# Moving some stores of a two-layer encoder kernel to ScalarE's queue, with three small re-stagings of its side work

## The chip, the cores and the metric

One core of one Trainium2 chip. The metric is the device time of one execution in microseconds (us), as the median of the runs shown.

## The reference

Two residual layers and a final RMSNorm over 1024 tokens of 1024 channels, all in fp32. Cut to what matters:

```python
for l in range(DEPTH):                       # 2
    h = rms_norm(x, norm_g[l])
    proj = h @ w_in[l]                       # 1024 x 6912
    qA, kA, vA, zA, uB, vB, zB, qM, zM, g_logits = split(proj)
    yA = gqa_axial_attention(qA, kA, vA, ...) * silu(zA)      # 8 query heads, 2 key heads, rotary
    yB = chunked_spatial_gating(uB, vB, ...) * silu(zB)       # layer norm, 128 x 128 mixing
    mem_n = rms_norm(mem, mem_norm_g[l])                      # 256 memory rows
    yM = memory_cross_attention(qM, mem_n, w_mem_kv[l]) * silu(zM)
    up = einsum('bsnw,nwd->bsnd', stack([yA, yB, yM]), w_br[l])
    x = x + sum(sigmoid(g_logits) * up, axis=2) @ w_out[l]
return rms_norm(x, final_g)
```

## The kernel before

Every large product is made of three fp32r matmuls (`mm3`, lines 122 to 124): each operand is split by ScalarE (a cast, the high part) and by VectorE or GpSimd (a subtraction, the low part). `split_w` (lines 164, 165) does this for weights, `split` (132, 133) for activations, `turn` (127) is a transpose on TensorE.

**Opening.** For each layer, `memory` norms 256 memory rows (L150, L152), turns them in four groups of four (two for each half of the rows), splits the results into `mTh` and `mTl`, multiplies by the key and value weights and stores the result in DRAM. Each group of turns takes a PSUM bank from `psT`, a pool of two; `psM` and `psA` are one bank each and are not used at this point. The token rows are normed and turned in between.

**Input projection** (`in_proj`). 27 column blocks of 256, each as seven products of 12 matmuls (a Winograd form of Strassen's scheme), 189 products in a written order. The weight operands are made seven products ahead (`AHEAD`); a block's weights are one load of 1 MB (`get_raw`). A block's results go through `use`, which is of a kind for each block: the last 12 blocks are gate logits (`logit`: a tanh on ScalarE, L405, and a store to `g_d`, 256 KB, four for each block); queries of the memory branch (`parts`) are stored in two parts to `qm_d`.

**Side work.** Between the products, `in_proj` resumes generators at given product numbers: `side` is a list of (start, generator), and a `yield n` means "go on n products later"; at most two generators are resumed behind one product. `qkv(L, tt)`, one for each of eight blocks of 128 rows, starts at 27 + 9 tt: it loads queries and keys from `proj_d`, turns them 4 products later (copies L560, L565), applies norm and rotary positions, splits (casts L586, L589 on ScalarE, subtractions L592, L594 on VectorE), turns the keys (copy L601, two stores of 128 KB to `k_d`), and one product later turns both groups of queries (copy L610 and a store of 256 KB to `qs_d` for each). The two groups and the keys share the two `psT` banks. `spatial(L, tt)` starts at 103 + 9 tt: it loads `vt` and `uz`, and 4 products later turns `vt` and goes through layer norm (copy L656), mixing and gating.

**After the projection.** Eight products before its end `cross` begins to load for the memory attention: keys and values (`kv_d`) and the queries of the first unit (`qm_d`); then come the loads of `yb_d` (4 MB), the keys and values of the other heads and the queries of the second unit. Its score matmuls are L766, L767 and L769. Then follow attention, the three branches (L723 multiplies by a gate that is loaded from `g_d`) and the output projection.

**What sets the order.** TensorE's order is the program's. The other engines' queues are ordered by a scheduler at build time, by readiness and priority (`tc.high_priority` raises it); buffers come from pools, of which `b2` has 18 and is used by nearly all side work and stores. Every DMA, load or store, is issued by `dma` on SyncE's queue (L106), in order: one that waits holds those behind it.

Of the kernel before, what the change touches and what calls it, by code (L numbers as in the profile page):

```python
# [28 lines left out]
NT = T // P  # L29
# [21 lines left out]
def trunk(ctx, tc, x_in, mem, norm_g, w_in, q_norm_g, k_norm_g, sg_ln_g, sg_ln_b, w_s, b_s,  # L51
          mem_norm_g, w_mem_kv, w_br, w_out, final_g, rope_t, out):
    nc = tc.nc
# [51 lines left out]
    def dma(out, in_):  # L105
        nc.sync.dma_start(out=out, in_=in_)  # L106

    eye = b2()[:, :P]
    make_identity(nc, eye)
    identr = const.tile([P, P], F32R, name="identr")  # L110
# [69 lines left out]
    def memory(l):  # L180

        gb = wt((P, D), F32)
        rows = slab((P, 2, D), F32)
        dma(rows[:, 0], mem[0, :P])
        dma(gb, mem_norm_g[l].partition_broadcast(P))
        dma(rows[:, 1], mem[0, P:2 * P])
        yield
        for mt in range(2):
            rms_rows(rows[:, mt], gb)
        mTh, mTl = slab((P, KT, MEM)), slab((P, KT, MEM))  # L190
        for mt in range(2):
            for i in range(2):
                pt = psT()
                for j in range(4):
                    turn(pt[:, j * P:(j + 1) * P], rows[:, mt, (4 * i + j) * P:(4 * i + j + 1) * P])
                m = slice(mt * P, (mt + 1) * P)
                k = slice(4 * i, 4 * i + 4)
                split(mTh[:, k, m], mTl[:, k, m], pt.rearrange("p (k t) -> p k t", k=4))
        yield
        for n in range(4):  # L200
            raw = raw_kv.pop(0)
            get_kv()
            W = [split_w(raw[:, i:i + 2], nc.vector if i % 4 else nc.gpsimd) for i in range(0, KT, 2)]
            for j in range(2):
                ps = psB()[:, :256]
                c = slice(j * P, (j + 1) * P)
                for kt in range(KT):
                    wh, wl = W[kt // 2]
                    if n < 2:
                        mm3(ps, wh[:, kt % 2, c], wl[:, kt % 2, c], mTh[:, kt], mTl[:, kt], kt == 0, kt == KT - 1)  # L210
                    else:
                        mm3(ps, mTh[:, kt, c], mTl[:, kt, c], wh[:, kt % 2], wl[:, kt % 2], kt == 0, kt == KT - 1)
                s = b2(F32R, (P, 2, 256))
                split(s[:, 0], s[:, 1], ps)
                if n < 2:
                    dma(kv_d[l][2 * n + j, :, :2].rearrange("p a m -> p a m"), f32(s))
                else:
                    for h in range(2):
                        dma(kv_d[l][2 * (n - 2) + h, :, 2:, c], f32(s[:, :, h * P:(h + 1) * P]))
            yield  # L220
# [139 lines left out]
    def blocks(L):  # L360

        def silu2(z):
            t = b2()
            nc.scalar.activation(t, z, AF.Tanh, scale=0.5)
            nc.vector.scalar_tensor_tensor(out=t, in0=t, scalar=1.0, in1=z, op0=ALU.add, op1=ALU.mult)
            return t

        def keep(dst):
            def use(j, th, z, bank):
                if bank:  # L370
                    t = b2()
                    nc.scalar.copy(t, z)
                    z = t
                dma(dst[j][:, half(th)], z)
            return use

        def gate(dst):
            def use(j, th, z, bank):
                dma(dst[j][:, half(th)], silu2(z))
            return use  # L380

        def both(dst):
            got = {}

            def use(j, th, z, bank):
                got[j, th] = z
                if (0, th) in got and (1, th) in got:
                    a = silu2(got[1, th])
                    u = got[0, th]
                    (nc.gpsimd if th else nc.vector).tensor_tensor(out=a, in0=a, in1=u, op=ALU.mult)  # L390
                    dma(dst[:, half(th)], a)
            return use

        def parts(dst):
            def use(j, th, z, bank):
                h, lo = b2(F32R), b2(F32R)
                split(h, lo, z, lo=nc.vector if bank else nc.gpsimd)
                dma(dst[j][:, 0, half(th)], f32(h))
                dma(dst[j][:, 1, half(th)], f32(lo))
            return use  # L400

        def logit(dst):
            def use(j, th, z, bank):
                t = b2() if bank else z
                nc.scalar.activation(t, z, AF.Tanh, scale=0.5)  # L405
                dma(dst[j][:, half(th)], t)
            return use

        out = [(K0, V0, keep(L.proj[4:6]))]
        out += [(Q0 + i * 256, Q0 + i * 256 + P, keep(L.proj[2 * i:2 * i + 2])) for i in range(2)]  # L410
        out += [(UB0 + f * P, ZB0 + f * P, both(L.uz[f])) for f in range(4)]
        out += [(VB0 + i * 256, VB0 + i * 256 + P, keep(L.proj[6 + 2 * i:8 + 2 * i])) for i in range(2)]
        out += [(ZA0 + i * 256, ZA0 + i * 256 + P, gate(L.za[2 * i:2 * i + 2])) for i in range(2)]
        out += [(QM0 + i * 256, QM0 + i * 256 + P, parts(L.qm[2 * i:2 * i + 2])) for i in range(2)]
        out += [(ZM0 + i * 256, ZM0 + i * 256 + P, gate(L.zm[2 * i:2 * i + 2])) for i in range(2)]
        out += [(G0 + i * 256, G0 + i * 256 + P, logit(L.g[2 * i:2 * i + 2])) for i in range(12)]
        return out
# [131 lines left out]
    def qkv(L, tt):  # L549

        t = slice(tt * P, (tt + 1) * P)
        qt, kt = b2(F32, (P, 4, P)), b2(F32, (P, 2, P))
        dma(qt, L.proj[0:4, :, t].rearrange("f p t -> p f t"))
        dma(kt, L.proj[4:6, :, t].rearrange("f p t -> p f t"))
        yield 4
        pt = psT()
        for f in range(2):
            turn(pt[:, f * P:(f + 1) * P], kt[:, f])
        kr = b2()
        nc.scalar.copy(kr[:, :256], pt[:, :256])  # L560
        pt = psT()
        for f in range(4):
            turn(pt[:, f * P:(f + 1) * P], qt[:, f])
        qr = b2()
        nc.scalar.copy(qr, pt)  # L565
        yield 1
        v = kr[:, P:2 * P].rearrange("p (g d) -> p g d", g=2)
        vs = b2(F32R, (P, 2, 2, 64))
        nc.scalar.copy(vs[:, :, 0], v)
        tabk, tabq = tabs[0]  # L570
        tmp = b2()
        k = Rope(kr[:, :P], tabk, 2, tt, tmp[:, :P], tmp[:, P:2 * P])
        q = Rope(qr, tabq, 8, tt, b2(), b2())
        k.begin()
        q.begin()
        yield 1
        nc.vector.tensor_tensor(out=vs[:, :, 1], in0=v, in1=f32(vs[:, :, 0]), op=ALU.subtract)
        dma(L.v[:, :, tt], f32(vs).rearrange("p g s d -> p g (s d)"))
        q.turn()
        k.turn()  # L580
        yield 1
        q, k = q.end(), k.end()
        yield 1
        ks = b2(F32R, (P, 2, 2, 2, 64))
        for s in range(2):
            nc.scalar.copy(ks[:, :, 0, s], k)  # L586
        qs = [b2(F32R, (P, 4, 2, 64)) for _ in range(2)]
        for g in range(2):
            nc.scalar.copy(qs[g][:, :, 0], q[:, 4 * g:4 * g + 4])  # L589
        yield 1  # L590
        for s in range(2):
            nc.vector.tensor_tensor(out=ks[:, :, 1, s], in0=k, in1=f32(ks[:, :, 0, s]), op=ALU.subtract)  # L592
        for g in range(2):
            nc.vector.tensor_tensor(out=qs[g][:, :, 1], in0=q[:, 4 * g:4 * g + 4], in1=f32(qs[g][:, :, 0]), op=ALU.subtract)  # L594
        yield 1
        pt = psT(F32R)
        for g in range(2):
            for i in range(2):
                turn(pt[:, (2 * g + i) * P:(2 * g + i + 1) * P], ks[:, g, i].rearrange("p s d -> p (s d)"), identr)
        o = b2(F32R)  # L600
        nc.scalar.copy(o, f32(pt))  # L601
        for g in range(2):
            dma(L.k[g, :, :, t], f32(o[:, g * 256:(g + 1) * 256]).rearrange("p (i t) -> p i t", i=2))
        yield 1
        for g in range(2):
            pt = psT(F32R)
            for h in range(4):
                turn(pt[:, h * P:(h + 1) * P], qs[g][:, h].rearrange("p s d -> p (s d)"), identr)
            o = b2(F32R)
            nc.scalar.copy(o, f32(pt))  # L610
            dma(L.qs[g, tt], f32(o))

# [19 lines left out]
    def spatial(L, tt):  # L634
# [1 line left out]
        vt, uz = b2(F32, (P, 4, P)), b2(F32, (P, 4, P))  # L636
        dma(vt, L.proj[6:10, :, t].rearrange("f p t -> p f t"))
        dma(uz, L.uz[:, :, t].rearrange("f p t -> p f t"))
        yield 4
        gbb, wsT, bs = spat[0]  # L640
        v = psT()
        for f in range(4):
# [429 lines left out]
    for l in range(DEPTH):  # L1072
# [1 line left out]
        side = [(4, tables(l))]  # L1074
        side += [(27 + 9 * tt, qkv(L, tt)) for tt in range(NT)]
        side += [(95, spatial_consts(l))]
        side += [(103 + 9 * tt, spatial(L, tt)) for tt in range(NT)]
        xatt = cross(L, lambda y: start_m(y))
        in_proj(L, H, between, side, lambda: next(xatt))
        between = {}  # L1080
# [129 lines left out]
```

## Time and profile before

| | |
|---|---|
| runs shown | 2153.57, 2148.07, 2150.33 us |
| median | 2150.33 us |
| the profiled execution, its own time | 2158.11 us |
| its span, first to last instruction | 2156.3 us |
| mean granted TensorE clock | 0.984 of full speed |
| TensorE busy | 2054.3 us of the span |

PE is TensorE, PEld its weight loads, DVE VectorE, ACT ScalarE, POOL GpSimd, SP SyncE (SPq its queue). L106 is line 106 of the kernel. Busy time of pipelined matmuls is modelled. In an answer on waits, the releaser named is the one that came last by the profile.

### The profile page before, as it was taken

Reading aid. Unit: us, or ns where it says so; the run is one execution under the profiler, and the core shown is the slowest. Engines: PE = TensorE matmul, PEld = TensorE weight load, DVE = VectorE, ACT = ScalarE, POOL = GpSimd, SP = SyncE. Lnnn points to the kernel's source line nnn. Section 1 sums busy time; section 2 is a strip of 40 time slices with the busy share of each in tenths; the row PEclk is TensorE's granted clock in tenths of the full one; section 3 lists DMA queues with packets and bytes.
Section 4 is the critical chain, followed back from the end, with each engine's and each line's share of the span. In section 5 each row is a group of like instructions: output and inputs, shape, how many; then the busy total and the mean of one; then the engine's idle time right before and its main releaser. Section 6 shows DMA issues by size and latency. Waiting matters only on the chain.

```text
span 2156.3 us, 29973 instructions
## 1 busy us (share of the span) xinstructions
PE 2054.3 (95%) x10464; PEld 1727.1 (80%) x10464; DVE 1384.8 (64%) x2014; ACT 1021.7 (47%) x2053; POOL 1138.7 (53%) x1068
## 2 busy tenths in 40 slices
PE   6899999999999999999987999999999999999998
PEld 5778787788887788888876888778888788888786
DVE  6866766666654677786258476676666357777733
ACT  5533344434433577784233244444334346778522
POOL 4666566555552445656237556655555235566542
PEclk9999999999999999999998999999999999999999
DMA  8543344544457511114432344544454752111332
GB/s 293 171 125 104 113 161 149 186 130 149 152 173 268 184 55 40 59 60 152 132 132 70 118 137 140 175 160 150 134 159 159 256 184 89 53 51 63 108 127 79
DMA packets 240711, 290.98 MB, mean 135 GB/s; under 512 B 13360, under 2 KB 155696, under 8 KB 239792
## 3 DMA queue, kind: packets, MB, share of 16 engines
q1 hardware_dynamic: 240560, 289.07, 40.5%
q8 instruction: 83, 1.36, 0.3%
q14 instruction: 68, 0.56, 0.1%
HBM read 196.74 MB, written 92.27 MB: 134 GB/s over the span
## 4 chain that ended last, share of the span: by engine, by line
PE 77%; DVE 9%; ACT 4%; issue 4%; DMA 3%; POOL 3%; SPq 0%; POOLq 0%; ACTq 0%; DVEq 0%
PE psB L123 13%; PE psB L122 13%; PE psB L124 13%; PE psT L127 7%; PE psM L122 5%; PE psM L124 5%; PE psM L123 4%; PE psA L896 4%; PE psA L122 2%; PE psA L124 2%; PE psA L123 2%; PE psS L865 2%; PE psS L866 2%; POOL wt L165 1%; DVE b L133 1%
## 5 line engine op out<-in xcount | busy, mean ns | idle before, releaser
L122 PE MATMUL psB<-s,wt 128*128 128x512 f32 (+1 forms) x1272 | 501.7, 394 | 8.2 <-ACT b L312 8.1
L124 PE MATMUL psB<-s,wt 128*128 128x512 f32 (+1 forms) x1272 | 495.3, 389 | 2.3 <-DVE wt L165 1.8
L123 PE MATMUL psB<-s,wt 128*128 128x512 f32 (+1 forms) x1272 | 495.4, 389 | 2.1 <-POOL s L133 1.2
L165 POOL TENSOR_TENSOR wt<-b,wt 128x512 fp32r<-128x512 f32 x216 | 304.8, 1415 | 281.6 <-ACT wt L164 256.1
L165 POOL TENSOR_TENSOR wt<-raw,wt 128x512 fp32r<-128x512 f32 x234 | 327.7, 1407 | 180.8 <-ACT wt L164 170.5
L122 PEld LDWEIGHTS psB<-s,wt 128*128 128x128 f32 x1272 | 243.6, 192 | 56.7 <-ACT b L312 9.4
L124 PEld LDWEIGHTS psB<-s,wt 128*128 128x128 f32 x1272 | 242.9, 191 | 51.9 <-DVE wt L165 2.0
L123 PEld LDWEIGHTS psB<-s,wt 128*128 128x128 f32 x1272 | 243.3, 191 | 50.2 <-POOL s L133 2.4
L164 ACT CAST wt<-b 128x512 fp32r<-128x512 f32 x216 | 133.0, 621 | 269.2 <-DVE b L279 81.6
L164 ACT CAST wt<-raw 128x512 fp32r<-128x512 f32 x274 | 167.3, 623 | 160.2 <-PE psB L124 88.5
L127 PE MATMUL psT<-identr,s 128*128 128x128 f32 x1184 | 182.4, 280 | 53.1 <-DVE b L259 13.3
L305 DVE TENSOR_TENSOR b<-psB,b 128x512 f32<-128x512 f32 x162 | 111.2, 686 | 181.3 <-PE psB L124 174.1
L133 DVE TENSOR_TENSOR b<-psT,b 128x512 fp32r<-128x512 f32 x288 | 193.7, 686 | 50.3 <-ACT b L132 47.3
L875 POOL TENSOR_SCALAR s<-s,sums 128x1024 f32<-128x1024 f32 x128 | 145.1, 1135 | 134.4 <-DVE sums L874 121.8
L122 PE MATMUL psM<-s,wt 128*128 128x512 f32 x472 | 194.2, 412 | 0.3
L127 PEld LDWEIGHTS psT<-identr,s 128*128 128x128 f32 x1184 | 137.6, 143 | 67.1 <-issue 31.0
L124 PE MATMUL psM<-s,wt 128*128 128x512 f32 x472 | 185.9, 394 | 0.0
L123 PE MATMUL psM<-s,wt 128*128 128x512 f32 x472 | 185.6, 393 | 0.0
L132 ACT CAST b<-psT 128x512 fp32r<-128x512 f32 x288 | 166.0, 585 | 36.2 <-PE psT L127 31.9
L896 PEld LDWEIGHTS psA<-b,s 128*128 128x128 f32 x1024 | 150.9, 189 | 23.5 <-ACT b L904 6.6
L896 PE MATMUL psA<-b,s 128*128 128x256 f32 x1024 | 167.9, 286 | 1.8 <-ACT b L904 0.8
L868 DVE TENSOR_REDUCE nm<-psS 128x1 f32<-128x1024 f32 x128 | 155.4, 1214 | 14.5 <-PE psS L866 14.1
(173 smaller groups left out, 3825.5 us busy)
## 6 DMA issues: line engine op xcount, KB each, us to landing
raw<-in_w_in_dram SPq DMA_DIRECT2D x46, 1024.0 KB, 5.5
g_d<-b SPq DMA_DIRECT2D x96, 256.0 KB, 3.1
b<-g_d SPq DMA_DIRECT2D x96, 256.0 KB, 5.5
raw<-in_w_in_dram SPq DMA_DIRECT2D x24, 512.0 KB, 5.2
raw<-in_w_br_dram SPq DMA_DIRECT2D x12, 1024.0 KB, 5.2
proj_d<-b SPq DMA_DIRECT2D x40, 256.0 KB, 2.1
raw<-in_w_mem_kv_dram SPq DMA_DIRECT2D x8, 1024.0 KB, 7.2
b<-proj_d SPq DMA_DIRECT2D x32, 256.0 KB, 3.7
```

Source lines behind the costliest of these rows:

```text
L122: pe(nc.tensor.matmul(ps, sh, mh, start=start, stop=False, skip_group_check=skip))
L123: pe(nc.tensor.matmul(ps, sh, ml, start=False, stop=False, skip_group_check=skip))
L124: pe(nc.tensor.matmul(ps, sl, mh, start=False, stop=stop, skip_group_check=skip))
L127: pe(nc.tensor.transpose(out, in_, ident if idn is None else idn))
L132: nc.scalar.copy(h, src)
L133: lo.tensor_tensor(out=l, in0=src, in1=f32(h), op=ALU.subtract)
L164: tc.stamp_issue_order_token(nc.scalar.copy(w[:, 0], raw).ins, "cast")
L165: (lo or nc.gpsimd).tensor_tensor(out=w[:, 1], in0=raw, in1=f32(w[:, 0]), op=ALU.subtract)
L305: nc.vector.tensor_tensor(out=o, in0=ps, in1=t, op=ALU.add)
L868: nc.vector.tensor_reduce(out=nm, in_=S, axis=AX.X, op=ALU.max, negate=True)
L875: nc.gpsimd.tensor_scalar(out=p, in0=p, scalar1=sums, scalar2=1.0, op0=ALU.mult, op1=ALU.mult)
L896: pe(nc.tensor.matmul(acc[:, :256], V[:, g, 2 * c + j], pv[:, j * 256:(j + 1) * 256], start=c + i + j == 0, stop=c == 3 and i + j == 2))
```

## The change

`put_out` issues a DMA on ScalarE's queue. The stores of the gate logits, of the keys and of the turned queries go through it. In `memory`, the turns of the second half of the rows take `psM` and `psA` instead of `psT`, and all four splits have a raised priority. In `qkv`, the second group of queries is turned one product behind the first. `spatial` starts two products earlier and waits two products longer between its loads and its turns.

```diff
+    def put_out(out, in_):
+
+        nc.scalar.dma_start(out=out, in_=in_)
+
...
         for mt in range(2):
             for i in range(2):
-                pt = psT()
+                pt = psT() if mt == 0 else (psM, psA)[i]()
                 for j in range(4):
                     turn(pt[:, j * P:(j + 1) * P], rows[:, mt, (4 * i + j) * P:(4 * i + j + 1) * P])
                 m = slice(mt * P, (mt + 1) * P)
                 k = slice(4 * i, 4 * i + 4)
-                split(mTh[:, k, m], mTl[:, k, m], pt.rearrange("p (k t) -> p k t", k=4))
+                with tc.high_priority(offset=200):
+                    split(mTh[:, k, m], mTl[:, k, m], pt.rearrange("p (k t) -> p k t", k=4))
...
                 nc.scalar.activation(t, z, AF.Tanh, scale=0.5)
-                dma(dst[j][:, half(th)], t)
+                put_out(dst[j][:, half(th)], t)
...
         for g in range(2):
-            dma(L.k[g, :, :, t], f32(o[:, g * 256:(g + 1) * 256]).rearrange("p (i t) -> p i t", i=2))
+            put_out(L.k[g, :, :, t], f32(o[:, g * 256:(g + 1) * 256]).rearrange("p (i t) -> p i t", i=2))
         yield 1
...
                 turn(pt[:, h * P:(h + 1) * P], qs[g][:, h].rearrange("p s d -> p (s d)"), identr)
             o = b2(F32R)
             nc.scalar.copy(o, f32(pt))
-            dma(L.qs[g, tt], f32(o))
+            put_out(L.qs[g, tt], f32(o))
+            yield 1
...
         dma(uz, L.uz[:, :, t].rearrange("f p t -> p f t"))
-        yield 4
+        yield 6
...
-        side += [(103 + 9 * tt, spatial(L, tt)) for tt in range(NT)]
+        side += [(101 + 9 * tt, spatial(L, tt)) for tt in range(NT)]
```

## Rows read from the trace of the kernel before

**Rows 1.** The page, part 1: busy time, share of the span, instructions.
```profile
PE 2054.3 (95%) x10464; PEld 1727.1 (80%) x10464; DVE 1384.8 (64%) x2014; ACT 1021.7 (47%) x2053; POOL 1138.7 (53%) x1068
```
**Rows 2.** Busy time by stretch: us, PE, PEld, DVE, ACT, POOL, PEclk, DMA share, GB/s.
```profile
130.00:665.00 535.00, 526.02 (x2425) 435.04 (x2423) 336.01 (x505) 211.03 (x399) 290.85 (x234) 0.99 0.48 156
```
**Rows 3.** TensorE's waits, whole run: us in total, times, longest us.
```profile
PE psT L127 <- DVE s L133: 9.8, 3, 5.8
...
PE psT L127 <- ACT b L601: 6.5, 4, 1.7
PE psT L127 <- DMA b<-proj_d: 6.1, 2, 3.1
...
PE psT L127 <- DVE b L592: 3.3, 8, 0.7
PE psS L766 <- DMA b<-qm_d: 3.0, 2, 1.7
...
PE psS L769 <- DMA b<-qm_d: 2.1, 2, 1.3
```
**Rows 4.** Busy time by stretch: three of ten microseconds in layer 1.
```profile
349.00:359.00 10.00, 9.07 (x38) 7.46 (x39) 4.21 (x4) 4.88 (x11) 6.72 (x6) 0.83 0.79 249
667.00:677.00 10.00, 9.22 (x41) 7.29 (x41) 4.24 (x7) 4.04 (x12) 3.45 (x8) 0.83 0.64 215
387.00:397.00 10.00, 9.29 (x37) 7.66 (x38) 4.41 (x9) 5.08 (x11) 4.87 (x4) 0.83 0.37 134
```
**Rows 5.** Timeline of TensorE: start us, us, instruction, idle time before it.
```profile
349.93 0.53 PE L127 MATMUL psT<-identr,b 128*128 128x128 f32 x4 [1.60 <-ACT b L601]
```
**Rows 6.** Timeline of ScalarE around the same turn.
```profile
347.76 0.62 ACT L132 CAST b<-b 128x512 fp32r<-128x512 f32 x1 [3.81 <-DVE b L305]
...
349.29 0.59 ACT L601 CAST b<-psT 128x512 fp32r<-128x512 f32 x1
```
**Rows 7.** Issues by tensor: ns min/median/max, first and last start.
```profile
L106 SPq DMA_DIRECT2D g_d<-b x96: 319/332/572, 427.8 to 1700.2; - x96
...
L106 SPq DMA_DIRECT2D k_d<-b x32: 524/613/1532, 210.0 to 1450.7; - x32
...
L106 SPq DMA_DIRECT2D qs_d<-b x32: 319/398/1432, 213.8 to 1453.5; - x32
```
**Rows 8.** Timeline of SyncE at the end of layer 1's projection.
```profile
657.42 0.39 SPq L106 DMA_DIRECT2D s<-kv_d  x1
659.68 3.04 SPq L106 DMA_DIRECT2D g_d<-b  x2
662.77 0.92 SPq L106 DMA_DIRECT2D b<-qm_d  x2
```
**Rows 9.** Busy time by stretch, just before those loads.
```profile
655.00:660.00 5.00, 5.00 (x24) 4.14 (x23) 1.38 (x2) 1.26 (x2) 0.00 (x0) 1.00 1.05 389
```
**Rows 10.** Timeline of SyncE before the wait for proj_d.
```profile
377.12 0.38 SPq L106 DMA_DIRECT2D raw<-in_w_in_dram  x1
...
379.24 1.20 SPq L106 DMA_DIRECT2D b<-proj_d  x2
```
**Rows 11.** Timeline around the first spatial block of layer 1.
```profile
419.23 0.56 SPq L106 DMA_DIRECT2D b<-uz_d  x1
...
429.21 0.60 PE L127 MATMUL psT<-identr,b 128*128 128x128 f32 x4
```
**Rows 12.** Timeline of the opening.
```profile
11.03 2.18 ACT L164 CAST wt<-raw 128x512 fp32r<-128x512 f32 x4 [1.86 <-DMA raw<-in_w_mem_kv_dram]
...
15.13 1.27 DVE L133 TENSOR_TENSOR s<-psT,s 128x512 fp32r<-128x512 f32 x2
...
15.86 1.97 PE L127 MATMUL psT<-identr,s 128*128 128x128 f32 x8 [5.82 <-DVE s L133]
...
17.63 0.69 DVE L133 TENSOR_TENSOR s<-psT,s 128x512 fp32r<-128x512 f32 x1 [1.23 <-ACT s L132]
```
**Rows 13.** SyncE's waits, whole run: us in total, times, longest us.
```profile
SPq L106 <- DMA b<-g_d: 10.6, 23, 1.5
```

## The prediction

> **What bounds the kernel now.** I read the page first, then the list of what TensorE waited for, then stretches, then the timeline around each wait. TensorE is busy for 2054.3 of 2156.3 us, the other engines for at most 64% [rows 1], so only time in which TensorE stands still, or runs at the lower of its two clock levels, can be won: 102 us of standing and some half-speed time. In the input projection of layer 1, TensorE is busy 526.0 of 535 us [rows 2]; the 189 products of that stretch take 535 / 189 = 2.83 us each, side work included. So the projection has 9 us to win in a layer, and the rest of the idle time lies in places that the diff mostly does not touch. The waits that lie near the edited lines are these [rows 3]: the turns of queries and keys wait 6.5 us in total for the copy L601 (4 times), 6.1 us for a load from proj_d (twice), 3.3 us for the subtraction L592 (8 times); the first scores of the memory attention wait 3.0 + 2.1 us for loads from qm_d (twice each, once a layer); the turns of rows at the opening wait 9.8 us for the subtraction L133 (3 times).
> A stop costs more than its own length where the clock falls behind it. In the ten microseconds from 349, from 667 and from 387 the mean granted clock is 0.83 [rows 4], that is 2.4 GHz with 1.2 GHz for a third of the stretch: 10 x (1 - 0.83) = 1.7 us of work lost each time. The same three stretches of layer 2 read the same, six in all.
>
> **The change, part by part.**
> Queries in two stages. Both query groups are now turned right behind each other, one product after the keys. The timeline shows the second group starting at 349.93 after 1.60 us of waiting for L601 [rows 5]: it takes the psT bank that the keys had, and L601, their copy out of it, ran only at 349.29, because ScalarE had stood 3.81 us at L132 in front of it for a sum that comes out of the running product [rows 6]. A product later that copy is done: it ends at 349.29 + 0.59 = 349.88, and the second group would be due at about 349.93 - 1.60 + 2.83 = 351.2. All four waits of this kind go, 6.5 us. Two of the four are followed by the lower clock (349 and its twin in layer 2), so 2 x 1.7 = 3.4 us more. Sum -9.9 us. Late next is the copy of the first group, which nobody turns behind until the next block of rows.
> Stores on ScalarE. What it removes from SyncE's queue is 96 + 32 + 32 issues; GpSimd's queue is not touched. What it adds to ScalarE is not in the trace, since ScalarE issues nothing there. The nearest rows are SyncE's own issues of the same transfers: median 0.33, 0.61 and 0.40 us, longest 1.53 us [rows 7]. I take the medians: 96 x 0.33 + 32 x 0.61 + 32 x 0.40 = 64 us, 32 us a layer, on an engine that in the projection is busy 211 of 535 us [rows 2]; the ends are zero (the idle time swallows it) and 160 x 1.53 = 245 us, which would still leave it busy 334 of 535 us. A gain on ScalarE itself is excluded, as it had no such work. Each store waits there for its own copy or tanh, and behind it stand weight casts, the next tanh, the copy of a block's first product and the copies of the side work. Casts are made seven products ahead (some 20 us), so 0.3 to 0.6 us more in front of them is covered; uncovered are the copies that a turn needs one product later (L560, L565, L586, L656). I put 1 us in total on those.
> Where the freed queue pays is the end of each projection. SyncE issued the load of key and value rows at 657.42, then stood at two gate stores (659.68, 3.04 us for both, the second one issued when the last tanh was done) and came to the loads of the second unit's queries only at 662.77 [rows 8]; these are what TensorE waits for at 665 and 667. Without the stores in front, nothing between 657.8 and 662.77 holds them, so they move up by up to 5 us, against waits of at most 1.7 and 1.3 us [rows 3]. All 5.1 us should go, with the lower clock behind them in both layers, 3.4 us: -8.5 us. Late next would be the gate load that stands behind them on SyncE, and it moves up with them. Against this speaks the DMA share in that stretch, 1.05 at 389 GB/s [rows 9]: the transfers themselves are at their limit there, and moving an issue does not make them shorter.
> The Trainium skill, DMA: Bandwidth & Descriptors, section Issuing engines are not separate DMA queues, says that transfers started by different engines run on the same 16 DMA engines, and that a second issuer saves sequencer time alone. Taken by itself that rule puts this term at zero and the sum at -8.5 us instead of -17.
> I still take the whole term, because the row shows an issue that waited its turn in a queue, not a transfer that was slow.
> In the rest of the projection the same move buys nothing: the one load that TensorE waits for, the queries and keys of the last block of rows, is issued at 379.24 behind a 1 MB weight load at 377.12 [rows 10], which does not move, as it is no store. I leave its 6.1 us and the lower clock behind it, from 387 [rows 4], where they are. It may grow: the key and query stores were queued behind it on SyncE and now run beside it; two of them (128 and 256 KB) at 389 GB/s are 1 us, so +1 us in all, with -9.5 us (both waits and both clock drops gone) and +3 us as the ends.
> Spatial loads. They start two products earlier (101) and are awaited at the same one (107). The load of uz at 419.23 was already 10 us ahead of the turn at 429.21 [rows 11], and the waits for proj_d [rows 3] are those of the queries, not of this. Zero; the price is two buffers of the b2 pool held two products longer, which the seven products of lead cover. If that cover is gone, VectorE waits for a buffer, for which I allow 0 to 2 us.
> Memory rows in four banks. At the opening ScalarE does four weight casts from 11.03 before it copies the first turns; VectorE's two subtractions follow at 15.13, and the second eight turns, for want of a bank, start at 15.86 after 5.82 us; the third subtraction ends at 17.63 + 0.69 = 18.32 [rows 12]. With two banks of their own the second turns can start when their rows are normed, and the products wait for the subtractions alone. If ScalarE's order stays, these run from 15.13 one behind the other, and the third ends at 15.13 + 1.27 + 0.69 = 17.1, a gain of 1.2 us. If the raised priority puts the copies ahead of the casts, the most that can be won is the whole stop, 5.8 us. I take 2, near the lower end, since the row shows the casts starting when the weights land, which priority does not alter. With half a microsecond for the same wait at the second memory (the rest of the 9.8 us [rows 3] is for a bank that is not moved), -2.5 us. Nothing hides this stretch, so it is passed on; if a later load sets the pace, it is zero.
> Sum: -9.9 - 8.5 - 2.5 + 1 + 1 = -18.9 us; I keep -17, since a stop that goes tends to leave a little of itself at the next wait. The profiled execution took 2158.11 us, 1.8 over its span and 7.8 over the median of the runs, 2150.33; the saving lies in stops that every execution has, so it is taken off the median: 2133 us.
>
> **The rivals.**
> A, the bandwidth holds. The queries of the second unit arrive when the megabytes ahead of them are through, whoever issues. For it speaks the share of 1.05 [rows 9], against it that SyncE held them back for 5 us [rows 8]. Then -17 + 8.5 = -8.5: 2142 us.
> B, the change does not reach its waits: another wait takes the place of L601 (the same turns already wait 3.3 us for L592 [rows 3]) and the opening is set by weights. Then all that is left is noise around -2: 2148 us.
> C, the wait for proj_d goes as well, because with fewer issues SyncE is ahead of the weight load. Then -17 - 9.5: 2123.5 us. Against it: the weight load waits for its own buffer, not for a store.
> D, slower: ScalarE stands at its stores. SyncE is seen waiting for transfers to land before it may issue the next, 23 times behind gate loads, up to 1.5 us [rows 13], and it could afford that. If ScalarE has such a wait at the key and query stores, its copies for the next turns come late. It decides from the point where a turn's slack, one product or 2.83 us, is eaten. Priced at 1.5 us for each of 16 blocks of rows, 24 us, with the lower clock behind half of them, 8 x 1.7 = 14 us, less the -11 us of the other two parts: +27, 2177 us. Against it: ScalarE idles 60% of the projection.
>
> **How the numbers follow.** What a measurement here can tell from no change is about 0.3%, 6.5 us. Chances: the forecast 0.55 (its own range 2125 to 2140), A 0.18, B 0.13, C 0.07, D 0.07. Faster: 0.54 of the forecast, 0.14 of A, 0.07 of C, 0.75. Same: 0.01, 0.04 of A, 0.11 of B, 0.16. Slower: D and 0.02 of B, 0.09. The range goes from C's side, 2122, to B's, 2150; D and the ends of the unknown prices beyond stay out, under 2 in 10.
>
> **What would show it.** Right: no wait for L601 in TensorE's list; no wait for qm_d at the scores and a clock of 1.00 right behind them; the second eight turns at the opening before 13; ScalarE's issues near 0.3 to 0.6 us; the wait for proj_d still there twice. Wrong: the qm_d waits at their old size beside a DMA share of 1 (A), new waits of turns for L560, L565 or L586 with ScalarE idle in front of them (D), or the wait for proj_d gone (C).

## The result and the profile after

The changed kernel takes 2138.26 us (median of 4 runs, 2134.70 to 2139.88); the kernel before, beside it, 2151.55 (4 runs, 2148.07 to 2153.57). The ratio is 0.9932, with a 95% interval of 0.9917 to 0.9948: 14.6 us less, 11 to 18. (The quotient of the two medians shown is 0.9938, 13.3 us less; it lies inside that interval.) The measured time lies inside the forecast's own range of 2125 to 2140, 5 us above its 2133, and the sign agrees; the saving of 17 us was overrated by 2.4 us. One execution behind the experiments below, of the version with the queries alone (2301.64 us, at a mean granted clock of 0.846), was in a slower state and is left out of its ratio.

The profiled execution took 2139.88 us, with a span of 2138.1, against 2156.3 before: 18.2 us. First the page: busy time, share of the span and instructions of each engine, and the new DMA queue (packets, MB, share of the 16 engines).
```profile
PE 2047.3 (96%) x10464; PEld 1722.2 (81%) x10464; DVE 1382.8 (65%) x2014; ACT 1021.6 (48%) x2053; POOL 1134.8 (53%) x1068
...
q10 hardware_dynamic: 27136, 37.76, 5.0%
```
Beside [rows 1], TensorE is busy 7.0 us less with the same 10464 products, and stands still 2138.1 - 2047.3 = 90.8 us instead of 102.0. So the 18.2 us are 11.2 us of stops and 7.0 us of pace. The two parts fare differently below. Queue q10 is new: the 160 stores that ScalarE now issues.

TensorE's list of waits, whole run (us in total, times, longest us); lines stand 4 to 6 lower than before, so L131 is the old L127, L137 the old L133, L597 the old L592.
```profile
PE psT L131 <- DMA b<-proj_d: 7.7, 3, 3.3
...
PE psT L131 <- DVE b L597: 3.5, 8, 0.7
PE psT L131 <- DVE s L137: 3.4, 1, 3.4
...
PE psB L127 <- DVE s L137: 1.8, 1, 1.8
PE psM L131 <- DVE s L156: 1.4, 1, 1.4
PE psB L126 <- ACT s L136: 1.3, 1, 1.3
PE psB L126 <- ACT wt L168: 1.0, 1, 1.0
```
Against [rows 3]: the 6.5 us for the copy of the keys (old L601, now L606) and the 5.1 us for loads from qm_d are gone without remainder. Of the 9.8 us of the opening's turns 3.4 are left, a stop at 44.8 us for a bank that the change does not move; in place of the other 6.4 stand 5.5 us of new waits, for the rows, the copies, the weights and the subtraction (1.4, 1.3, 1.0, 1.8). Two waits for weight subtractions behind them (0.55 us at 25.89 and 1.78 at 28.65) have become one of 0.85, so that the opening stands 2.4 us less in all. The wait for proj_d has grown from 6.1 to 7.7 us.

**The turns of queries.** TensorE and ScalarE around one block of rows (start us, us, instruction, idle time before it). The turns are, in this order, the last three of the keys, the first group of queries and the second group; L606 is the copy of the keys.
```profile
342.86 0.46 PE L131 MATMUL psT<-identr,b 128*128 128x128 f32 x3 [0.30 <-DVE b L597]
...
345.97 0.46 PE L131 MATMUL psT<-identr,b 128*128 128x128 f32 x4
...
349.08 0.46 PE L131 MATMUL psT<-identr,b 128*128 128x128 f32 x4
```
```profile
345.86 0.62 ACT L136 CAST b<-b 128x512 fp32r<-128x512 f32 x1 [3.81 <-DVE b L310]
...
347.38 0.59 ACT L606 CAST b<-psT 128x512 fp32r<-128x512 f32 x1
348.00 1.28 ACTq L110 DMA_DIRECT2D k_d<-b  x2
```
ScalarE still stands 3.81 us for the sum, as in [rows 6], and its copy of the keys still comes late: it ends at 347.38 + 0.59 = 347.97, 2 us after the first group was turned. But the second group of queries, which needs that bank, now comes a product later, at 349.08, 1.1 us after the copy's end, and waits for nothing.

**The end of the projection.** SyncE's queue there, and the stretch of ten microseconds before and after the scores (us, busy time of PE, PEld, DVE, ACT, POOL, PEclk, DMA share, GB/s):
```profile
632.80 6.74 SPq L106 DMA_DIRECT2D s<-yb_d  x4
639.83 2.86 SPq L106 DMA_DIRECT2D s<-kv_d  x1
642.82 3.38 SPq L106 DMA_DIRECT2D b<-qm_d  x2
```
```profile
647.00:657.00 10.00, 10.00 (x52) 8.50 (x51) 3.47 (x5) 1.90 (x3) 0.00 (x0) 1.00 1.05 401
657.00:667.00 10.00, 9.57 (x51) 7.97 (x50) 4.87 (x9) 5.87 (x20) 5.23 (x10) 1.00 0.59 208
```
In [rows 8] two gate stores stand between the load of key and value rows and the loads from qm_d. Now the loads follow directly. They are issued from 642.82 to 646.20; the first scores start at 653.46, nearly 11 us after the first issue. Before, the first scores started at 661.77, 1 us ahead of the issue at 662.77. So the loads have moved up by some 12 us against the scores, not by the 5 that the prediction allowed. The reason stands further up in the queue of before: not only the last two gate stores held loads there, but three of the four loads of `yb_d`, and the load of key and value rows, came right behind a gate store as well. The loads of `yb_d` were issued at 641.04, 643.78, 648.46 and 651.94, where they now go in one row from 632.80. The last of them before:
```profile
651.52 0.32 SPq L106 DMA_DIRECT2D g_d<-b  x1
651.94 0.39 SPq L106 DMA_DIRECT2D s<-yb_d  x1
657.01 0.32 SPq L106 DMA_DIRECT2D g_d<-b  x1
```
The DMA share is still 1.05 as in [rows 9], and the loads arrive in time all the same.

**ScalarE's issues** (ns min/median/max, first and last start):
```profile
L110 ACTq DMA_DIRECT2D g_d<-b x96: 326/326/393, 420.5 to 1688.8; - x96
L110 ACTq DMA_DIRECT2D k_d<-b x32: 520/587/765, 207.9 to 1440.3; - x32
L110 ACTq DMA_DIRECT2D qs_d<-b x32: 325/326/353, 211.2 to 1444.2; - x32
```
They cost what SyncE's medians in [rows 7] said, or a little less. One row shows ScalarE standing at a store:
```profile
654.38 0.63 ACT L410 ACTIVATE b<-b 128x512 f32<-128x512 f32 x1 [2.09 <-DVE b L310]
656.60 0.33 ACTq L110 DMA_DIRECT2D g_d<-b  x1
```
The tanh ends at 655.01, its store is issued 1.6 us later; what it stood for, the rows do not name. Nothing urgent is behind it there.

**The opening** (timeline):
```profile
10.85 2.18 ACT L168 CAST wt<-raw 128x512 fp32r<-128x512 f32 x4 [1.91 <-DMA raw<-in_w_mem_kv_dram]
11.23 1.12 PE L131 MATMUL psM<-identr,s 128*128 128x128 f32 x4 [1.36 <-DVE s L156]
...
16.16 0.68 DVE L137 TENSOR_TENSOR s<-psM,s 128x512 fp32r<-128x512 f32 x1
16.89 0.58 PE L127 MATMUL psB<-s,wt 128*128 128x256 f32 x1 [1.77 <-DVE s L137]
```
The second turns start at 11.23 instead of 15.86 [rows 12]. The four weight casts still stand ahead of the copies, and the third subtraction, for which the second product waits, ends at 16.16 + 0.68 = 16.84 instead of 18.32 (the prediction worked out 17.1 for it).

### The profile page after: what moved, and what is told of

The parts are those of the page before. It is cut to its first block, busy times and chain, and to the rows that moved or that the text cites. A ratio compares the mean times of both kernels' runs of the same rounds, so it can differ in the third digit from the quotient of the medians.

```text
span 2138.1 us, 29870 instructions
## 1 busy us (share of the span) xinstructions
PE 2047.3 (96%) x10464; PEld 1722.2 (81%) x10464; DVE 1382.8 (65%) x2014; ACT 1021.6 (48%) x2053; POOL 1134.8 (53%) x1068
## 4 chain that ended last, share of the span: by engine, by line
PE 76%; DVE 10%; ACT 4%; DMA 4%; issue 3%; POOL 2%; ACTq 0%; SPq 0%; POOLq 0%; DVEq 0%
PE psB L126 13%; PE psB L127 13%; PE psB L128 13%; PE psT L131 6%; PE psM L126 5%; PE psM L128 4%; PE psM L127 4%; PE psA L902 4%; PE psA L126 2%; PE psA L128 2%; PE psA L127 2%; PE psS L871 2%; PE psS L872 2%; DVE b L137 1%; ACT s L879 1%
## 5 line engine op out<-in xcount | busy, mean ns | idle before, releaser
L127 PE MATMUL psB<-s,wt 128*128 128x512 f32 (+1 forms) x1272 | 495.1, 389 | 4.7 <-POOL s L137 2.5
L127 PEld LDWEIGHTS psB<-s,wt 128*128 128x128 f32 x1272 | 243.6, 191 | 51.8 <-POOL s L137 3.7
L137 DVE TENSOR_TENSOR b<-psT,b 128x512 fp32r<-128x512 f32 x288 | 193.9, 687 | 50.3 <-ACT b L136 47.1
L131 PE MATMUL psT<-identr,s 128*128 128x128 f32 x1168 | 178.4, 278 | 45.8 <-DVE b L264 12.8
L127 PE MATMUL psM<-s,wt 128*128 128x512 f32 x472 | 184.9, 392 | 0.0
L131 PEld LDWEIGHTS psT<-identr,s 128*128 128x128 f32 x1168 | 134.6, 142 | 58.9 <-issue 30.3
```

What stands on the lines that cost most here:

```text
L127: pe(nc.tensor.matmul(ps, sh, ml, start=False, stop=False, skip_group_check=skip))
L131: pe(nc.tensor.transpose(out, in_, ident if idn is None else idn))
L137: lo.tensor_tensor(out=l, in0=src, in1=f32(h), op=ALU.subtract)
```

## The experiments

In each, the kernel before ran beside it on the same chip (23 or 26 runs). Percentages, and differences in us that stand beside a ratio, are from the ratios, which are not quotients of the medians. First the change was taken apart.

**All stores to ScalarE, nothing else.**
```diff
-                dma(dst[j][:, half(th)], t)
+                put_out(dst[j][:, half(th)], t)
-            dma(L.k[g, :, :, t], f32(o[:, g * 256:(g + 1) * 256]).rearrange("p (i t) -> p i t", i=2))
+            put_out(L.k[g, :, :, t], f32(o[:, g * 256:(g + 1) * 256]).rearrange("p (i t) -> p i t", i=2))
-            dma(L.qs[g, tt], f32(o))
+            put_out(L.qs[g, tt], f32(o))
```


> Only the three kinds of stores go to ScalarE's queue; queries, spatial loads and memory banks as before. Theory (a blocked queue): SyncE reaches the loads of the second unit's queries some 15 us before the first scores need them, both qm_d waits (5.1 us in the two layers) and the lower clock behind them are gone, the four waits for L601 stay at 6.5 us: 8 to 9 us less than before, ratio 0.996. Rival (the bandwidth holds): the DMA share at the end of the projection is 1.0 as before and the qm_d waits stay within 1 us of their old size: ratio 1.000. Rival (ScalarE stands at its stores): the qm_d waits go, but the waits for L601 grow above 6.5 us since its bank is copied later, ratio 0.998 to 1.002.

Measured: 2145.79 us, ratio 0.9965 (0.9953 to 0.9978). TensorE's waits:
```profile
PE psT L131 <- DMA b<-proj_d: 7.7, 2, 4.1
PE psT L131 <- ACT b L605: 6.5, 4, 1.6
```
No wait for qm_d is left, the copy of the keys (here L605) is awaited as before, proj_d more than before. That is what the theory expected.

**Queries in two stages, nothing else.**
```diff
             dma(L.qs[g, tt], f32(o))
+            yield 1
```


> Only the second group of queries is turned one product later. Theory: the four waits for L601 (6.5 us) are gone, with two lower-clock stretches behind them (3.4 us), less about 1 us of a new wait elsewhere: 8 to 10 us less, ratio 0.996. Rival (the time is only passed on): TensorE comes to the last block of queries earlier and waits there longer for proj_d, by about as much as it won; the sum of the waits for L601 and proj_d falls by less than 3 us: ratio 0.999.

Measured: 2144.98 us, ratio 0.9965 (0.9953 to 0.9978).
```profile
PE psS L767 <- DMA b<-qm_d: 3.7, 2, 2.0
...
PE psT L127 <- ACT b L586: 3.5, 4, 1.0
PE psT L127 <- DMA b<-proj_d: 3.2, 2, 2.3
```
No wait for the copy of the keys. The rival had it passed on to proj_d; that wait fell too, from 6.1 to 3.2. The waits for qm_d stay (3.7 and 1.2 us). A little came back as waits for the copy L586, 3.5 us against 1.8 in the kernel before.

**Memory rows in four banks with the raised priority, nothing else.**
```diff
-                pt = psT()
+                pt = psT() if mt == 0 else (psM, psA)[i]()
-                split(mTh[:, k, m], mTl[:, k, m], pt.rearrange("p (k t) -> p k t", k=4))
+                with tc.high_priority(offset=200):
+                    split(mTh[:, k, m], mTl[:, k, m], pt.rearrange("p (k t) -> p k t", k=4))
```


> Only the memory rows: four banks and raised priority. Theory: the first product at the opening starts about 3 us earlier, but three quarters of that is lost again before the token rows, and some 2 us are left at the end: ratio 0.999. Rival (all of it is passed on): 3.5 to 4 us less, ratio 0.998. Rival (the gain is nothing but where the low clock happens to fall): first product 3 us earlier, and no difference left by 90 us: ratio 1.000.

Measured: 2147.81 us, ratio 0.9982 (0.9972 to 0.9993), 3.9 us. The wait of the opening's turns shrinks as it does in the whole change, to the stop for the bank that is not moved (the copy of the keys is awaited for 6.5 us as before):
```profile
PE psT L127 <- DVE s L133: 3.7, 1, 3.7
```
The measured ratio lies between theory (0.999) and rival (0.998), and its interval holds both.

**The two halves of that: banks without priority, priority without banks.**

> Only the four banks for the memory rows, without the raised priority of their splits. Theory: the banks are all of it, since ScalarE casts weights first with the priority or without: the first product starts at 14 to 15 us, ratio 0.998 as with both. Rival (the priority does it): first product after 16 us and ratio 0.9995 to 1.000.

> Only the raised priority of the memory rows' splits, banks as before. Theory: ScalarE casts weights first all the same, the second eight turns still wait near 5.8 us: ratio 1.000. Rival (the priority carries half of the gain at the opening, as the difference of 0.0009 between banks with it and without it says): ratio 0.999, and low-clock time at the opening shorter by 3 us or more.

Measured: the banks alone 2150.26 us, ratio 0.9991 (0.9982 to 1.0001), with the first product at 14.40 (with the priority 14.37, before 17.65); the priority alone 2152.55, ratio 0.9986 (0.9970 to 1.0003), with the stop of 5.6 us at the opening still there. The banks make the earlier start; what the priority is worth the two intervals can't tell.

**Spatial loads earlier, nothing else.**
```diff
-        yield 4
+        yield 6
-        side += [(103 + 9 * tt, spatial(L, tt)) for tt in range(NT)]
+        side += [(101 + 9 * tt, spatial(L, tt)) for tt in range(NT)]
```


> Only the spatial loads two products earlier. Theory: no wait of TensorE hung on them, ratio 1.000 within its interval, the same list of waits as before within 1 us. Rival (buffers): the two buffers held longer make VectorE wait and TensorE's waits grow by over 2 us: ratio 1.001 or more. Rival (the loads were late after all): some of the proj_d waits (6.1 us) go, ratio 0.998.

Measured: 2151.78 us, ratio 1.0000 (0.9991 to 1.0010): zero. All three waits that the other parts touch are at their old size (L601 6.5 us and proj_d 6.1 us, word for word as in [rows 3], and qm_d), so this run also serves as a second look at what follows such stops: its wait for qm_d, and stretches with the mean granted clock in the third column from the right.
```profile
PE psS L766 <- DMA b<-qm_d: 5.1, 2, 2.9
```
```profile
349.00:359.00 10.00, 9.96 (x49) 8.38 (x50) 3.82 (x5) 4.59 (x9) 7.04 (x5) 1.00 0.77 237
385.00:395.00 10.00, 8.89 (x35) 7.36 (x36) 4.41 (x9) 5.19 (x11) 4.52 (x4) 0.83 0.37 130
665.00:675.00 10.00, 8.48 (x40) 7.39 (x41) 3.65 (x7) 3.93 (x12) 3.12 (x8) 0.83 0.69 236
```
Behind the stop for the copy of the keys, 1.59 us long here, the clock is 1.00, where [rows 4] had 0.83. Behind proj_d (3.00 us) and qm_d (2.95 us) it falls again in this layer; in layer 2 it is 1.00 behind the proj_d stop of 3.11 us at 1422.63.

**Which stores carry it: the gates alone, the keys and queries alone.** The edits are the first pair, or the other two pairs, of the first diff.

> Of the stores, only those of the gate logits go to ScalarE's queue. Theory: they alone stood in front of the loads of the second unit's queries, so both qm_d waits (5.1 us) go as they did with all three kinds of store moved; the waits for proj_d stay at 6 us, not 7.7, since keys and queries still queue behind that load on SyncE: 7 to 9 us less, ratio 0.996 to 0.997. Rival (the effect came from the keys and queries): qm_d waits stay, ratio 1.000.

> Of the stores, only those of keys and queries go to ScalarE's queue. Theory: nothing is won by them; the qm_d waits stay at about 5 us, the waits for proj_d grow from 6.1 to about 7.7 us since these stores now share the DMA engines with the load: ratio 1.000 to 1.001. Rival (a freer SyncE queue in the projection pays): waits for proj_d below 6 us, ratio 0.998 or less.

Measured: gates alone 2143.33 us, ratio 0.9954 (0.9939 to 0.9968); keys and queries alone 2154.47, ratio 1.0012 (1.0001 to 1.0023). The wait for proj_d with the gates moved:
```profile
PE psT L131 <- DMA b<-proj_d: 5.5, 2, 2.8
```
and the waits for loads with keys and queries moved:
```profile
PE psT L131 <- DMA b<-proj_d: 7.8, 3, 4.0
...
PE psS L770 <- DMA b<-qm_d: 3.3, 2, 1.9
```
Two waits for qm_d at another score line bring the 3.3 us to 4.3, against 5.1 before. The gate stores carry the whole gain of the move; the other 64 stores cost 0.12%, just clear of the noise. With the gates moved the stretch in front of the scores is as full as ever, and the waits for qm_d are gone:
```profile
655.00:660.00 5.00, 5.00 (x24) 4.14 (x23) 1.38 (x2) 1.26 (x2) 0.00 (x0) 1.00 1.05 408
```

**A version from that: the changed kernel with keys' and queries' stores back on SyncE.**
```diff
-            put_out(L.k[g, :, :, t], f32(o[:, g * 256:(g + 1) * 256]).rearrange("p (i t) -> p i t", i=2))
+            dma(L.k[g, :, :, t], f32(o[:, g * 256:(g + 1) * 256]).rearrange("p (i t) -> p i t", i=2))
-            put_out(L.qs[g, tt], f32(o))
+            dma(L.qs[g, tt], f32(o))
```


> The changed kernel with the stores of keys and queries back on SyncE; gates stay on ScalarE. Theory: these stores on ScalarE cost about 0.1% alone, and so here: the waits for proj_d fall from 7.7 to 6 us or less, ratio to before 0.991 to 0.993, at or below the changed kernel's. Rival (it is even inside the whole change): waits for proj_d stay above 7 us and the ratio is within 0.0005 of the changed kernel's.

Beside it the changed kernel itself ran once more:

> The changed kernel once more, unaltered, beside the next three. Theory (a fixed saving and a part that differs from execution to execution): the same waits of TensorE within 0.5 us each, but stretches of lower clock at other places or fewer of them than in the first profile; ratio 0.992 to 0.994. Rival (the clock falls at the same stops each time): the same lower-clock stretches, and so 1412 to 1420 again at half clock.

Measured: 2136.06 us, ratio 0.9912 (0.9887 to 0.9937), against 2139.97 and 0.9923 (0.9896 to 0.9950) for the changed kernel. By medians 3.9 us better, but the intervals overlap. The wait for proj_d is 4.8 us here,
```profile
PE psT L131 <- DMA b<-proj_d: 4.8, 2, 2.5
```
and in the changed kernel's second profile 7.8. That second profile was expected to place its low-clock stretches elsewhere, and that expectation failed: most stand within a microsecond or two of the first profile's, among them the one behind the wait for proj_d in layer 2 (first the one profile, then the other):
```profile
1411.00:1421.00 10.00, 6.92 (x22) 5.76 (x23) 3.19 (x5) 2.74 (x6) 3.94 (x3) 0.66 0.54 189
```
```profile
1411.00:1421.00 10.00, 6.64 (x21) 5.56 (x22) 3.31 (x4) 2.76 (x6) 3.69 (x3) 0.66 0.54 190
```

**An attempt on proj_d: queries and keys loaded two products earlier in the changed kernel.**
```diff
-        yield 4
+        yield 6
-        side += [(27 + 9 * tt, qkv(L, tt)) for tt in range(NT)]
+        side += [(25 + 9 * tt, qkv(L, tt)) for tt in range(NT)]
```


> The changed kernel, with the loads of queries and keys for each block of rows started two products earlier (25 + 9 tt) and awaited 6 products later instead of 4. Theory: the load of the last block now stands in front of the 1 MB weight load on SyncE, the 7.7 us of waits for proj_d are gone and some of the lower clock behind them (up to 5 us): 8 to 12 us less than the changed kernel, ratio to before about 0.988 to 0.990. Rival (buffers): two buffers held two products longer where the memory queries are stored make VectorE or ScalarE wait, other waits of TensorE grow, and the ratio stays at 0.993 or above.

Measured: 2135.78 us, ratio 0.9917 (0.9903 to 0.9930). The wait for proj_d is gone, and its place is taken:
```profile
PE psT L131 <- DVE b L597: 6.7, 9, 1.7
...
PE psT L131 <- ACT b L591: 3.5, 2, 1.8
...
PE psT L131 <- ACT b L615: 1.3, 2, 1.1
```
Against the changed kernel (3.5 us for L597, 1.8 for L591, 0.2 for L615) that is 6.0 us of new waits for 7.7 removed. Theory and rival both saw part of it, and the ratio lies between theirs; the gain over the changed kernel is about 2 us, within the intervals.

**Both (these stores back on SyncE, loads two products earlier), and the keys turned two products behind their subtraction.** The two `dma` lines of the version above belong to the edit as well.
```diff
-        side += [(27 + 9 * tt, qkv(L, tt)) for tt in range(NT)]
+        side += [(25 + 9 * tt, qkv(L, tt)) for tt in range(NT)]
...
-        yield 4
+        yield 6
...
-        yield 1
+        yield 2
```


> The kernel with gates alone on ScalarE, loads of queries and keys two products earlier, and the keys turned two products behind the subtraction L597 instead of one. Theory: the waits for proj_d (7.7 us in the changed kernel) and those for L591 and L597 (10.2 us with the earlier loads alone) are gone from the projection: ratio to before 0.987 to 0.990. Rival (the side work only moves along): other waits of turns take their place, ratio 0.9915 or above.

Measured: 2150.75 us, ratio 0.9990 (0.9972 to 1.0008): the whole gain is given back. The waits for proj_d, L597 and L591 are gone, and this one stands in their place, with one of its sixteen from the timeline:
```profile
PE psT L131 <- ACT b L615: 22.5, 16, 3.3
```
```profile
330.37 0.70 PE L131 MATMUL psT<-identr,b 128*128 128x128 f32 x6
...
331.89 0.57 ACT L615 CAST b<-psT 128x512 fp32r<-128x512 f32 x1
...
332.51 0.66 PE L131 MATMUL psT<-identr,b 128*128 128x128 f32 x4 [1.45 <-ACT b L615]
```
A block starts every nine products. The last group of queries is now turned 15 products after its block's start, the next block's first turns come 9 + 6 = 15 after it: the same product. Three turns want two banks, and the third waits for the copy of the queries. In the changed kernel the two stand 12 and 13 products behind and do not meet.

## Why the prediction was right, and where it was off

The kernel became faster, for the stated reasons. Term by term, with the run that has that part alone:

| term | forecast, us | measured, us (interval) |
|---|---|---|
| queries in two stages | -9.9 | -7.5 (-10 to -5) |
| stores on ScalarE, all | -8.5 + 1 + 1 = -6.5 | -7.5 (-10 to -5) |
| of these, gates | -8.5, +1 | -9.9 (-13 to -7) |
| of these, keys and queries | +1 | +2.6 (0 to +5) |
| memory rows | -2.5 | -3.9 (-6 to -2) |
| spatial loads | 0 | 0 (-2 to +2) |
| whole | -17 | -14.6 (-18 to -11) |

**The waits were right.** Those for L601 and qm_d went whole, on the terms named: a product later the copy is done; without the gate stores the loads follow at once, and move further than was worked out, since gate stores ahead of those two held loads as well. ScalarE's issues cost the medians of SyncE's. The casts at the opening stayed ahead of the copies. Rival A, the bandwidth, fell: the DMA share stayed at 1.05 and the wait went. The gates alone were worth 0.46%, with the share as before, because an urgent load was queued behind stores that waited for their data. The Trainium skill, DMA: Bandwidth & Descriptors, section Issuing engines are not separate DMA queues, holds that a second issuer saves only the sequencer time of starting a DMA, usually small beside the transfer. These runs agree as far as the transfers go; but what they gained was not the time of starting a store, 0.33 us. It was the time for which loads stood in SyncE's queue behind stores whose data were not ready: SyncE waited 219.3 us for the tanh L405 before, 73 times, and in the changed kernel never. Rival D was seen at most once (the store that stood 1.6 us at 656.60), where no turn follows. B and C did not come.

**No single run convicts a term.** Each forecast in the table lies inside the interval of its run, that of the whole too. Which of them were mis-sized can be read from the traces only.

**The clock term was mis-sized.** It is "two of the four are followed by the lower clock", 3.4 us behind L601 and the same again behind qm_d, read in one execution and taken off the median. Seven other kernels of this record keep the four stops for the copy of the keys (1.57 to 1.69 us each). Behind 24 of these 28 stops the mean granted clock of the next ten microseconds is 1.00, behind 4 it is 0.83. By that rate an estimate of the term is 4/28 x 4 x 1.7 = 1.0 us instead of 3.4. Behind qm_d it holds better: in the six other kernels that keep those stops, 8 of 12 are followed by 0.83 to 0.85, 2.3 us instead of 3.4. The averages agree. The execution that I read had an unusually low clock: its mean granted clock over the span is 0.984, while the 72 runs of the kernel before beside the experiments average 0.9867, and the 10 runs of the changed kernel 0.9877. In busy time of some 2050 us, 0.004 between the two profiled executions is 8 us (the page shows 7.0), but 0.001 between the averages is 2 us. With the 11.2 us of stops that makes 13.2 us, beside the 13.3 between the medians. So the 18.2 us of the two spans overstate the change by some 5 us, and the 6.8 us of clock in the sum should have been 2 to 3.

**The proj_d term looks too small.** Against "+1 us in all" the run with keys and queries alone measured 2.6 (0 to 5): with these stores issued beside the load instead of behind it, its waits went from 6.1 to 7.8 us, and stayed at 5.5 with the gates alone. This half of the move worked against the change. The cause named, transfers that overlap, shows in the landing of that load. With the gates alone the key stores are issued at 379.15, 1.5 us after the load began to be issued (377.62); with keys and queries moved they are issued at 375.66, 0.2 us after it (375.46), and it takes longer to land in the last block of rows of layer 1 (first gates alone, then keys and queries alone):
```profile
DMA to landing us min/median/max: 7.3/7.5/7.8
```
```profile
DMA to landing us min/median/max: 8.2/8.4/8.7
```
In both layers the median is 8.3 to 8.8 us in the four profiles that have the key stores on ScalarE (all stores, keys and queries alone, and both profiles of the changed kernel), and 7.2 to 8.0 in the eight others with that load at its old place. The 1 us put on ScalarE's copies can't be told apart in any run.

**The opening was sized about right.** I kept 2 us and half a microsecond. The early start gave what was worked out (the second product at 16.89 instead of 18.38, 1.5 us), and the stops of the opening fell by 2.4 us. The 1000th matmul of TensorE starts at 219.76 before, at 217.62 with the whole change and at 217.68 with this part alone: 2.1 us. The 3.9 us of that run have an interval of 2 to 6; the traces show no cause for more than the 2.4.

**The near hit of the whole is partly luck.** The clock was overrated by some 4 us, the cost of the key and query stores underrated by about 1, and the 1.9 us taken off the sum by hand, for stops that leave a little of themselves, rest on no row.

The parts measured one by one sum to -7.5 - 7.5 - 3.9 = -18.9 us, the whole to -14.6. Part of the difference may be noise (each part is uncertain by 2 to 3 us). One part is seen, in one profile each: queries alone bring the wait for proj_d down to 3.2 us, with the stores added it is at 7.7.

## What to carry to other kernels

Move to another issuer only the stores that stand in a queue ahead of a load that is about to be needed; the other 64 here gained nothing and slowed a load beside which they then ran. Take stops off the median in full, but the lower clock behind them only at the rate at which several profiles show it, and ask first whether the execution that was read is a typical one: compare its mean granted clock with that of many runs. Before side work is moved by a few products, lay its period and its number of banks over the neighbouring block: a shift by a product or two gave back the whole gain.

## What the runs showed of the hardware

The lower clock does not follow a stop of a given length each time. Behind the copy of the keys, stops of some 1.6 us, it followed 2 of 4 in the profile of before and 4 of 28 in seven other kernels. Longer stops for proj_d were followed by a mean of 0.83 over ten microseconds in both layers of before (2.98 and 3.13 us); with the spatial loads alone by 0.83 in layer 1 (3.00 us) and 1.00 in layer 2 (3.11 us); in the changed kernel by 1.00 in layer 1 (3.24 us) and 0.72 in layer 2 (3.29 us). In two profiles of the changed kernel, taken in different sessions, the lower stretches fell at nearly the same places.

At the opening the 256-wide products of both kernels took 0.41 us each until 20.2 us and 0.28 us after it, whether the first one had started at 17.65 or at 14.53. In the run with the memory edit alone the slow pace lasted past 21 us:
```profile
21.15 0.41 PE L122 MATMUL psB<-s,wt 128*128 128x256 f32 x1
```
The trace's records of the granted clock begin at that moment: at 20.28 us before, at 20.29 in the changed kernel, at 22.12 in the run of this row. In all fourteen profiles the first record starts between 19.5 and 22.1 us, and the faster pace at most 0.12 us later. For the time ahead of the first record the views show 1.00 without a record, so that figure says nothing there. The pace itself, products 0.21 us apart and then 0.12, is close to what the lower level makes elsewhere (512-wide products behind 351 us of before are 0.43 us apart instead of 0.23). So TensorE probably ran at the lower level until then, though no record says so.

In the profiled execution of the changed kernel with keys' and queries' stores back on SyncE, a VectorE operation that takes 0.68 us in the median of the changed kernel took 7.33:
```profile
725.44 7.33 DVE L140 SCALAR_TENSOR_TENSOR s<-b,s 128x512 fp32r<-128x512 f32 x1 [0.70 <-ACT s L139]
```
GpSimd ran eight weight subtractions in a row beside it, from 722.27 for 9.95 us. TensorE lost 5.5 us to it; that execution, 2142.07 us, is 6 over the median of its kernel. Whether the two belong together stays open.
